# A two-layer decoder trunk on one core: first layer's parameter loads in three parts, weight sums started later

## The chip, the cores and the metric

One core of a Trainium2 chip. The metric is the device time of one execution in microseconds (us), as the median of several runs. A profile is one execution with the hardware profiler on. Its engines are PE (TensorE: matmuls and transposes), DVE (VectorE), ACT (ScalarE), POOL (GpSimd) and SP (SyncE, which here only issues transfers). Each of them works through its own queue in order and waits at the head of it for what its next instruction needs.

## The reference

Two layers, each with a residual connection, on x of 512 tokens by 1024 channels, all float32. One projection `w_in` feeds four groups; `w_out` joins them again.

```python
def hybrid_layer(x, positions, norm_g, w_in, ...):
    h = rmsnorm(x, norm_g)
    p = h @ w_in                                   # 1024 x 3488
    (cq, ckv, kr, g_a, c_h, c_b, c_c, g_b, sg_u, sg_v, g_c, mq, mk, mv, g_d) = jnp.split(p, offs, axis=-1)
    q  = rmsnorm(rmsnorm(cq, mla_q_norm_g) @ mla_w_uq, mla_q_g)          # 4 heads of 96
    kv = rmsnorm(ckv, mla_kv_norm_g) @ mla_w_ukv
    k_nope, k_rope = rmsnorm(..., mla_k_nope_g), rope(rmsnorm(kr, mla_k_rope_g))
    o_a = causal_attention_blocks(q, k, v_a)
    o_b = c_b * short_conv(c_c * c_h, conv_w)
    o_c = sg_u * (tril(sg_w) @ layernorm(sg_v, sg_ln_g, sg_ln_b) + sg_b)
    o_d = moba_attention(rope(rmsnorm(mq, moba_q_g)), rope(rmsnorm(mk, moba_k_g)), mv)
    y = concat([o_a * silu(g_a), o_b * silu(g_b), o_c * silu(g_c), o_d * silu(g_d)])
    return y @ w_out
```

## The kernel before

**Units.** The weights come in units of up to 128 x 1024 float32 (512 KB). `load_units` issues one transfer per unit on SP, in a fixed order: c0 to c3 (the columns cq, ckv and kr), uq, ukv, sq0 to sq3 (sg_v and mq), ga0, ga1 (a gate), kv0 to kv3 (mk and mv), su0, gc0, ch0, cc0 and so on. A unit lands in a raw buffer; there are two ordinary ones (`NRAW`), and c2, c3, uq, ukv and some later units use others, so sq0 gets the buffer of c0 and sq1 that of c1. `split_units` then splits each unit, half by half, in a high part (ACT, at times DVE) and a low part (DVE), and so frees the raw buffer. PE makes each product out of three matmuls (high x high, low x high, high x low). sq0 to sq2 are split into the tiles yTh and yTl, which are not otherwise used yet.

**Start.** In the first layer x is loaded in five pieces (`load_xk`), the last three of which `LOAD_HOOKS` puts behind the units c0 to c2. PE transposes it (xT), ACT scales it into hTh, DVE makes the low half hTl, and PE multiplies with c0 to c3 into cq (`c_first`). ACT also squares x for the norm (junk). The hook of ukv_0 calls `load_params(L0)`, which issues thirteen transfers for the first layer's small parameters: the gains cg (two), gq, gk, gr, lg, lb, dq, dk, the bias sgb and the convolution weights cw (three).

**Order.** All instructions are put out by a planner, `Order`, with a clock of its own: each chain of steps (`Chain`) asks to be resumed at a due time, and the steps of an engine go into its queue in the order in which the planner resumes them. Costs and due times are written in the code (`GT`, `MIXT`, `TS0` and others, in nanoseconds of that clock). On the chip only the order stays; when an instruction runs is decided by its queue and its semaphores. `scale`, which multiplies gq and dq by a constant on POOL, is due at `GT`, and `L.g_ev` tells the planner that both are done; `q_chain` and `mqk_chain` wait for it.

**Sums of output weights.** The last product of each layer (`seven`) is done with seven block products instead of eight, in the order b11, t3, b21, t4, t2, t1, b22. For that `t_sums` makes four sums of blocks of `w_out` in DRAM (t1 to t4), each in two halves: a copy, issued on SP, and a transfer that adds, issued on POOL.

```python
nc.sync.dma_start(z_src(l, n, j), z_src(l, a, j))
...
nc.gpsimd.dma_start(z_src(l, n, j), quad(l, b, j), accum_op=ALU.add, max_dma_last_dim=1024)
```

t1 and t3 come first, then t2 out of t1, then t4 out of t2. For the first layer it is started at `TS0`; for the second, after that layer's product sq. `load_units` loads t1 to t4 as units like any other, after they are made. The accumulators oz, ox and oy of the profile belong to this stage (oz: b11 and b21; ox: t3 and t4; oy: t2, t1, b22).

**Mix.** The spatial gate (`mix_chain`) has PE multiply the split of sg_w (wsh, wsl) with the normalized sg_v (vnh, vnl) into the tiles mp, between the matmuls of kv. ACT evicts them with the bias sgb into mix, which frees an accumulator of a pool of three.

Of the kernel before, what the change touches and what calls it, by code (L numbers as in the profile page):

```python
# [11 lines left out]
F32 = mybir.dt.float32  # L12
# [3 lines left out]
ALU = mybir.AluOpType  # L16
AX = mybir.AxisListType

P = 128
S = 512  # L20
NT = S // P
# [4 lines left out]
GW = 256  # L26
# [6 lines left out]
WSLACK = 0.0  # L33
AHEAD = 4
NWARM, FILL, FILLEND = 6, 0.9, 15000.0
MIXT, MIXLAG, ROWT, GT = 42000.0, 2000.0, 27000.0, 27000.0
KSPLIT, SQPOOL = 6, 700.0
PAIRS = {}
LOPRIO = -5
# [4 lines left out]
SEVEN = (0, 1)  # L44
K0, K1, KK = (2, 3, 0, 1), (4, 5, 6, 7), (0, 2, 3, 1)
ZPROD = ("b11", "t3", "b21", "t4", "t2", "t1", "b22")
TS0 = 36000.0
TAIL = ((0, 256), (256, 512))

C_CQ, C_KV, C_GA, C_CH, C_CB, C_CC, C_GB = 0, 256, 416, 672, 928, 1184, 1440  # L50
# [3 lines left out]
def dram(ap, offset, pattern):  # L54
    return bass.AP(tensor=ap.tensor, offset=ap.offset + offset, ap=pattern)
# [161 lines left out]
def hybrid_trunk(ctx: ExitStack, tc: tile.TileContext, x, positions, norm_g, w_c, w_f, w_t, w_o, mla_q_norm_g,  # L217
                 mla_w_uq, mla_kv_norm_g, mla_w_ukv, mla_q_g, mla_k_nope_g, mla_k_rope_g, conv_w,
                 sg_ln_g, sg_ln_b, sg_w, sg_b, moba_q_g, moba_k_g, out):
    nc = tc.nc  # L220
    V, A, G, PE = nc.vector, nc.scalar, nc.gpsimd, nc.tensor

    cst = ctx.enter_context(tc.tile_pool(name="cst", bufs=1))
    lay = ctx.enter_context(tc.tile_pool(name="lay", bufs=1))
# [13 lines left out]
    o = Order()  # L238
# [218 lines left out]
    LOAD_HOOKS = {}  # L457
# [103 lines left out]
    def bcast(src, offset, n, name):  # L561
        tl = lay.tile([P, n], F32, tag=name, name=name)
        nc.sync.dma_start(tl, dram(src, offset, [[0, P], [1, n]]))
        return tl
# [10 lines left out]
            L.ng.append(g)  # L575
        o.set(L.ng_ev, ch.t)

    def load_params(L):
        l = L.l
        L.cg = lay.tile([P, 384], F32, tag="cg_b", name="cg_b")  # L580
        nc.sync.dma_start(L.cg[:, 0:256], dram(mla_q_norm_g, l * 256, [[0, P], [1, 256]]))
        nc.sync.dma_start(L.cg[:, 256:384], dram(mla_kv_norm_g, l * 128, [[0, P], [1, 128]]))
        L.gq = bcast(mla_q_g, l * 96, 96, "gq_b")
        L.gk = bcast(mla_k_nope_g, l * 64, 64, "gk_b")
        L.gr = bcast(mla_k_rope_g, l * 32, 32, "gr_b")
        L.lg = bcast(sg_ln_g, l * GW, GW, "lg_b")
        L.lb = bcast(sg_ln_b, l * GW, GW, "lb_b")
        L.dq = bcast(moba_q_g, l * 64, 64, "dq_b")
        L.dk = bcast(moba_k_g, l * 64, 64, "dk_b")
        L.sgb = lay.tile([P, 4], F32, tag="sgb", name="sgb")  # L590
        nc.sync.dma_start(L.sgb, dram(sg_b, l * 512, [[1, P], [P, 4]]))
        L.cw = lay.tile([P, 2, 3], F32, tag="cw", name="cw")
        for j in range(3):
            nc.sync.dma_start(L.cw[:, :, j], dram(conv_w, (l * 3 + j) * GW, [[1, P], [P, 2]]))
        L.par_t = o.now + 4000.0
        L.ssq = lay.tile([P, NT, 3], F32, tag="ssq", name="ssq")
        L.krt = lay.tile([P, NT, 32], F32, tag="krt", name="krt")

        def scale():
            ch = Chain(o, L.par_t)  # L600
            yield from ch.pool(G.tensor_scalar, L.gq, L.gq, -(96 ** -0.5), None, op0=ALU.mult)
            yield from ch.pool(G.tensor_scalar, L.dq, L.dq, -0.125, None, op0=ALU.mult)
            o.set(L.g_ev, ch.t)
        o.spawn(scale(), None if L.l else GT, 2)

    layers = []
    for l in range(DEPTH):
        L = Layer()
        L.l = l
        L.ng_ev = Event()  # L610
        L.hT, L.hTh = [[Event(), Event()] for _ in range(NT)], [[Event(), Event()] for _ in range(NT)]
        if l:
            L.xss = [cst.tile([P, 4], F32, name=f"xss{t}_{l}") for t in range(NT)]
        L.qd = [Event() for _ in range(NT)]
        L.kd = [Event() for _ in range(NT)]
        L.stat = [Event() for _ in range(NT)]
        L.Vt, L.Mt, L.gates, L.gate_ev, L.MD = {}, {}, {}, {}, {}
        L.md_ev = {n: [Event() for _ in range(NT)] for n in ("mq", "mk", "mv")}
        L.vt_ev = [Event() for _ in range(NT)]
        L.y = [Event() for _ in range(KT)]  # L620
        L.xr = [Event() for _ in range(NT)]
        L.vn_ev = [Event() for _ in range(NT)]
        L.u, L.u_ev, L.b, L.b_ev = {}, {}, {}, {}
        L.mix_ev, L.mla_ev, L.QK_ev = Event(), Event(), Event()
        L.seven = l in SEVEN
        L.hT_free, L.p1, L.h_done, L.h = Event(), Event(), [Event(), Event()], {}
        L.s_done, L.g_ev = Event(), Event()
        L.s = {n: [Event() for _ in range(4)] for n in ("t2", "t1", "b22")}
        L.left, L.s4 = {}, [Event(), Event()]
        L.QK_taken = False  # L630
        L.torder = (2, 3, 0, 1) if l and layers[l - 1].seven else (0, 1, 2, 3)
        L.x = [None] * NT
        for n in ("ga0", "ga1", "gd0", "gd1"):
            L.gate_ev[n] = Event()
        for j in range(2):
            L.u_ev[j] = Event()
            L.b_ev[j] = [Event() for _ in range(3)]
        layers.append(L)
# [15 lines left out]
    def rv(i, t):  # L654
        return xv[:, i, t:t + 1]
# [505 lines left out]
    def mqk_chain(nm):  # L1161
        def f(L, t, a, t0, put):
            ch = Chain(o, t0)
            l = L.l
            gn = L.dq if nm == "mq" else L.dk
            if t == 0:
                L.MD[nm] = yield from ydS.get(ch, f"{nm}{l}", [P, NT, 4, 64], F32)
                o.set(L.md_alloc[nm], ch.t)
            yield from ch.wait(L.md_alloc[nm])
            dst = L.MD[nm]  # L1170
            a4 = a[:, 0:256].rearrange("p (h d) -> p h d", h=4)
            m = sm.tile([P, 8], F32, tag="m" if nm == "mq" else "mk", name=f"m{nm}{t}_{l}")
            yield from ch.act(A.activation, dst[:, t], a4, AF.Copy)
            put(ch)
            yield from head_sums(ch, m, dst[:, t], 64)
            if l == 0:
                yield from ch.wait(v_ev)
            yield from ch.pool(G.tensor_scalar, m[:, 0:4], m[:, 0:4], 64 * EPS if l else rv(RE64, t), 1.0 / 64,
                               op0=ALU.add, op1=ALU.mult)
            yield from pow_rstd(ch, m[:, 4:8], m[:, 0:4], 4)  # L1180
            yield from ch.wait(L.g_ev)
            for h in range(4):
                yield from ch.dve(V.scalar_tensor_tensor, dst[:, t, h, :], in0=dst[:, t, h, :],
                                  scalar=m[:, 4 + h:5 + h], in1=gn, op0=ALU.mult, op1=ALU.mult)
            yield from ch.wait(rope_ev)
            ce = cosT[:, t, :].rearrange("p (i two) -> p i two", two=2)[:, :, 0]
            se = sinT[:, t, :].rearrange("p (i two) -> p i two", two=2)[:, :, 0]
            yield from rope(ch, dst[:, t, :, 0:8], dst[:, t, :, 8:16], ce.unsqueeze(1).to_broadcast([P, 4, 8]),
                            se.unsqueeze(1).to_broadcast([P, 4, 8]), 4, 8, f"{nm}{t}{l}")
            o.set(L.md_ev[nm][t], ch.t)  # L1190
        return f
# [562 lines left out]
    L0 = layers[0]  # L1754

    def start():
        o.clk["D"] = 1000.0
        cw = Chain(o)
        for kp in range(KT // 2):
            xk[kp] = yield from v4S.get(cw, f"x{kp}_0", [P, NT, 2 * P], F32)  # L1760
        load_xk(0, 1)
        wp = yield from sS.get(cw, "warm")
        ones = one_box[0][:, 0:P].bitcast(F32)
        V.memset(ones, 1.0)
        A.activation(xsum[:, 0, 0:1], ones[:, 0:1], AF.Square, scale=D ** -0.5)
        o.fill = lambda: PE.matmul(wp[:, 0:P], ones, ones, start=True, stop=True)
        for _ in range(NWARM):
            o.fill()
        PE.transpose(wp[:, 256:256 + NT + KT], junk[0:NT + KT, P:2 * P], ident[0:NT + KT, 0:NT + KT])
        V.tensor_copy(pg, wp[:, 256:256 + NT + KT])  # L1770
        o.pe_end, o.fill_until = 3700.0, FILLEND
        o.clk["V"] = 3700.0

        def fill_end():
            o.fill_until = 0.0
            sS.put(Chain(o))
            return
            yield
        o.spawn(fill_end(), FILLEND, -9)
        LOAD_HOOKS["c0_0"] = (lambda: load_xk(2, 4),)  # L1780
        LOAD_HOOKS["c1_0"] = (lambda: load_xk(4, 6),)
        LOAD_HOOKS["c2_0"] = (lambda: load_xk(6, 8),)
        LOAD_HOOKS["ukv_0"] = (lambda: load_params(L0),)
        L0.par_t = 17500.0
        for u in order[:10]:
            u.wanted = True
        o.spawn(load_units(), None, 4)
        o.spawn(split_units(0, 4), None, LOPRIO)
        o.spawn(split_units(4, len(order)), None, 5)
        o.spawn(rope_tables(), 3700.0, 4)  # L1790
        o.spawn(x_stats(), None, 5)
        o.spawn(x_row(), ROWT, 5)
        o.spawn(main(), None, 10)
# [54 lines left out]
```

## Time and profile before

| | |
|---|---|
| median of 3 runs | 499.88 us (499.43 to 501.58) |
| the profiled execution | 501.79 us |
| its span in the profile | 500.1 us |
| PE busy | 489.4 us (98%) |
| DVE, ACT, POOL busy | 395.9, 314.9, 162.5 us |
| transfers | 81.98 MB, mean 164 GB/s |

How to read the rows: a row of the list of waits gives engine, line and tile that waited, what it waited for, the total in us, the count and the longest. A row of the timeline gives start, duration, engine, line, operation, output <- inputs; in brackets, how long the engine had been idle before it and what ended that. Line L174 is the planner's helper through which nearly all steps of ACT, DVE and POOL pass, L204 that of PE, L283 that of transfers, L343 and L349 are the copies and adds of the sums, L563, L581 to L594 the parameter loads. So one reads by tiles.

### The profile page before, as it was taken

How to read it: one execution, taken by the hardware profiler on the slowest of the kernel's cores; microseconds unless marked ns; L12 is line 12 of the kernel's file. 1: busy time of each engine (PE TensorE's matmuls, PEld its weight loads, DVE VectorE, ACT ScalarE, POOL GpSimd, SP SyncE). 2: the span in 40 equal slices, each digit the busy share in tenths (PEclk: the TensorE clock that was granted, in tenths of full speed). 3: DMA queues.
4: the chain of work that ended last, by engine and by line, in shares of the span. 5: the costliest groups of instructions: out<-in, count | busy, mean ns of one | idle time of the engine just before them, and what ended most of it. 6: DMA issues, size and time to landing. Idle time of an engine off the chain costs nothing.

```text
span 500.1 us, 7817 instructions
## 1 busy us (share of the span) xinstructions
PE 489.4 (98%) x2455; PEld 416.3 (83%) x2455; DVE 395.9 (79%) x1014; ACT 314.9 (63%) x918; POOL 162.5 (32%) x327
## 2 busy tenths in 40 slices
PE   9889998999999999999999999999999999999997
PEld 8888876888878888888888988888888888888886
DVE  3578995477989898789998789677888888665992
ACT  6679845475677776456656795565767776524640
POOL 7728993334532020010041478445441010000000
PEclk9989999999999999999999999999999999999999
DMA  8623639427457423796574323556439565474652
GB/s 276 217 85 128 235 91 230 139 85 126 150 147 183 133 65 130 237 306 198 175 269 133 118 84 128 210 128 126 101 111 252 190 158 117 147 274 173 223 179 98
DMA packets 37394, 81.98 MB, mean 164 GB/s; under 512 B 7133, under 2 KB 19433, under 8 KB 37097
## 3 DMA queue, kind: packets, MB, share of 16 engines
q1 hardware_dynamic: 28880, 73.09, 43.6%
q0 software_dynamic: 8448, 8.39, 11.1%
q8 instruction: 19, 0.31, 0.2%
q14 instruction: 23, 0.18, 0.1%
q10 hardware_dynamic: 24, 0.01, 0.0%
HBM read 73.61 MB, written 24.64 MB: 196 GB/s over the span
## 4 chain that ended last, share of the span: by engine, by line
PE 82%; DVE 7%; DMA 4%; ACT 3%; SPq 2%; issue 1%; POOL 0%; ACTq 0%
PE kv L204 9%; PE oy L204 6%; PE sq L204 5%; PE gb L204 4%; PE cb L204 4%; PE gd L204 4%; PE su L204 4%; PE oz L204 4%; PE ox L204 4%; PE cq L204 4%; PE cc L204 4%; PE gc L204 4%; PE ch L204 3%; PE sa L204 3%; PE ga L204 2%; PE sd L204 2%
## 5 line engine op out<-in xcount | busy, mean ns | idle before, releaser
L204 PE MATMUL kv<-whi_kv,hTh 128*128 128x512 f32 x64 | 27.0, 422 | 2.3 <-ACT mix L174 2.3
L174 ACT ACTIVATE pha<-pTa 128x512 fp32r<-128x512 f32 (+3 forms) x32 | 13.8, 435 | 23.9 <-PE pTa L204 23.9
L174 ACT ACTIVATE pd<-pd,mnd 128x256 f32<-128x256 f32 (+3 forms) x49 | 26.2, 545 | 2.9 <-DVE mnd L174 2.8
L174 ACT ACTIVATE pa<-pa,mna 128x256 f32<-128x256 f32 (+3 forms) x44 | 23.7, 549 | 4.4 <-DVE mna L174 4.4
L204 PE MATMUL kv<-wlo_kv,hTh 128*128 128x512 f32 x64 | 25.7, 401 | 0.0
L204 PE MATMUL kv<-whi_kv,hTl 128*128 128x512 f32 x64 | 25.6, 400 | 0.0
L174 ACT ACTIVATE phd<-pTd 128x512 fp32r<-128x512 f32 (+3 forms) x32 | 13.8, 435 | 17.4 <-PE pTd L204 17.3
L349 POOL DMA_DIRECT2D t<-in_w_o_dram x16 | 17.7, 1150 | 21.5 <-DMA t<-t 13.4
L204 PE MATMUL cq<-whi_c,hTh 128*128 128x416 f32 x64 | 21.8, 387 | 2.6 <-ACT hTh L174 2.6
L174 DVE TENSOR_TENSOR pla<-pTa,pha 128x512 fp32r<-128x512 f32 (+3 forms) x32 | 15.3, 482 | 9.4 <-ACT pha L174 9.3
L174 POOL TENSOR_TENSOR chs<-chs,rh 128x512 f32<-128x512 f32 x6 | 8.7, 1444 | 41.7 <-DVE chs L174 22.6
L174 DVE TENSOR_TENSOR wlo_t<-raw_t,whi_t 128x512 fp32r<-128x512 f32 x32 | 21.1, 681 | 0.0
L204 PE MATMUL cq<-wlo_c,hTh 128*128 128x416 f32 x64 | 20.6, 368 | 0.0
L204 PE MATMUL cq<-whi_c,hTl 128*128 128x416 f32 x64 | 20.4, 364 | 0.1
L174 ACT ACTIVATE whi_t<-raw_t 128x512 fp32r<-128x512 f32 x31 | 17.6, 618 | 3.8 <-DMA raw_t<-t 3.8
L174 DVE TENSOR_TENSOR pld<-pTd,phd 128x512 fp32r<-128x512 f32 (+3 forms) x32 | 15.5, 486 | 4.5 <-ACT phd L174 4.3
L204 PE MATMUL sq<-yTh,hTh 128*128 128x512 f32 x48 | 18.9, 393 | 0.0
L204 PE MATMUL sq<-yTh,hTl 128*128 128x512 f32 x48 | 18.7, 390 | 0.0
L204 PE MATMUL sq<-yTl,hTh 128*128 128x512 f32 x48 | 18.7, 389 | 0.0
L174 DVE CUSTOM_DVE_ANT_0 pa<-sa,maskb 128x512 f32<-128x512 f32 (+3 forms) x32 | 15.0, 482 | 3.6 <-PE sa L204 2.4
L174 DVE CUSTOM_DVE_ANT_0 pd<-sd,maskb 128x384 f32<-128x384 f32 (+3 forms) x32 | 15.2, 483 | 2.4 <-PE pTd L204 1.7
L174 DVE TENSOR_TENSOR wlo_b<-raw_b,whi_b 128x512 fp32r<-128x512 f32 x24 | 16.0, 684 | 1.2 <-ACT whi_b L174 1.2
(423 smaller groups left out, 1865.5 us busy)
## 6 DMA issues: line engine op xcount, KB each, us to landing
t<-in_w_o_dram POOLq DMA_DIRECT2D x16, 512.0 KB, 6.7
raw_t<-t SPq DMA_DIRECT2D x16, 512.0 KB, 4.2
raw_b<-in_w_o_dram SPq DMA_DIRECT2D x12, 512.0 KB, 4.4
raw_sq<-in_w_t_dram SPq DMA_DIRECT2D x8, 512.0 KB, 3.5
t<-in_w_o_dram SPq DMA_DIRECT2D x8, 512.0 KB, 5.3
raw_kv<-in_w_t_dram SPq DMA_DIRECT2D x8, 512.0 KB, 3.5
t<-t SPq DMA_DIRECT2D x8, 512.0 KB, 5.0
ys<-ysc SPq DMA_DIRECT2D x14, 256.0 KB, 5.7
```

What stands on the lines that cost most here:

```text
L174: f(*a, **k)
L204: f(*a, **k)
L349: nc.gpsimd.dma_start(z_src(l, n, j), quad(l, b, j), accum_op=ALU.add, max_dma_last_dim=1024)
```

## The change

`load_params` takes a part. For the first layer, part 0 (the two loads of cg) stays at ukv_0; part 1 (gr, gq, gk) is put behind the load of sq1, part 2 (lg, lb, dq, dk, sgb, cw) behind that of sq3. The scaling of gq stays due at `GT` (27 us of the planner's clock); the scaling of dq gets an event of its own, `gd_ev`, and is due at 42 us; `mqk_chain` waits for that. The second layer's parameters are loaded in one piece as before, with two chains for the scalings. `TS0` goes from 36 to 95 us.

```diff
-MIXT, MIXLAG, ROWT, GT = 42000.0, 2000.0, 27000.0, 27000.0
+MIXT, MIXLAG, ROWT, GT, GT2 = 42000.0, 2000.0, 27000.0, 27000.0, 42000.0
...
-TS0 = 36000.0
+TS0 = 95000.0
...
-    def load_params(L):
+    def load_params(L, part=None):
         l = L.l
...
+        if part in (None, 0):
+            L.cg = lay.tile([P, 384], F32, tag="cg_b", name="cg_b")
+            nc.sync.dma_start(L.cg[:, 0:256], dram(mla_q_norm_g, l * 256, [[0, P], [1, 256]]))
+            nc.sync.dma_start(L.cg[:, 256:384], dram(mla_kv_norm_g, l * 128, [[0, P], [1, 128]]))
+            L.ssq = lay.tile([P, NT, 3], F32, tag="ssq", name="ssq")
+            L.krt = lay.tile([P, NT, 32], F32, tag="krt", name="krt")
+            if l:
+                L.par_t = o.now + 4000.0
+        if part in (None, 1):
+            L.gr = bcast(mla_k_rope_g, l * 32, 32, "gr_b")
+            L.gq = bcast(mla_q_g, l * 96, 96, "gq_b")
+            L.gk = bcast(mla_k_nope_g, l * 64, 64, "gk_b")
+        if part in (None, 2):
+            L.lg = bcast(sg_ln_g, l * GW, GW, "lg_b")
+            L.lb = bcast(sg_ln_b, l * GW, GW, "lb_b")
+            L.dq = bcast(moba_q_g, l * 64, 64, "dq_b")
+            L.dk = bcast(moba_k_g, l * 64, 64, "dk_b")
+            L.sgb = lay.tile([P, 4], F32, tag="sgb", name="sgb")
+            nc.sync.dma_start(L.sgb, dram(sg_b, l * 512, [[1, P], [P, 4]]))
+            L.cw = lay.tile([P, 2, 3], F32, tag="cw", name="cw")
+            for j in range(3):
+                nc.sync.dma_start(L.cw[:, :, j], dram(conv_w, (l * 3 + j) * GW, [[1, P], [P, 2]]))
+
+        def scale(z, f, ev, t):
+            ch = Chain(o, t)
+            yield from ch.pool(G.tensor_scalar, z, z, f, None, op0=ALU.mult)
+            o.set(ev, ch.t)
+        if part in (None, 1):
+            o.spawn(scale(L.gq, -(96 ** -0.5), L.g_ev, L.par_t if l else GT), None, 2)
+        if part in (None, 2):
+            o.spawn(scale(L.dq, -0.125, L.gd_ev, L.par_t if l else GT2), None, 2)
...
-        L.s_done, L.g_ev = Event(), Event()
+        L.s_done, L.g_ev, L.gd_ev = Event(), Event(), Event()
...
-            yield from ch.wait(L.g_ev)
+            yield from ch.wait(L.gd_ev)
...
-        LOAD_HOOKS["ukv_0"] = (lambda: load_params(L0),)
+        LOAD_HOOKS["ukv_0"] = (lambda: load_params(L0, 0),)
+        LOAD_HOOKS["sq1_0"] = (lambda: load_params(L0, 1),)
+        LOAD_HOOKS["sq3_0"] = (lambda: load_params(L0, 2),)
```

More of the change, by code (lines that the diff above doesn't have):

```diff
@@ L576, in load_norm_gain @@
         o.set(L.ng_ev, ch.t)
-    def load_params(L):
+    def load_params(L, part=None):
         l = L.l
[L580 to L604, printed above, removed]
```

## The prediction

> **What bounds the kernel now.** I read the page's busy times and clock first, then who PE waited for, then the stretches around those waits.
>
> ```profile
> PE 489.4 (98%) x2455; PEld 416.3 (83%) x2455; DVE 395.9 (79%) x1014; ACT 314.9 (63%) x918; POOL 162.5 (32%) x327
> PEclk9989999999999999999999999999999999999999
> PE cq L204 <- ACT hTh L174: 2.6, 1, 2.6
> PE kv L204 <- ACT mix L174: 2.3, 1, 2.3
> PE warm L1766 <- DVE ones L1764: 1.1, 1, 1.1
> ```
>
> TensorE is busy for 489.4 of 500.1 us, so nothing outside its queue matters unless it makes PE wait or slows it. Only two waits of the whole run are longer than that of the warm-up at the start (1.1 us): one on the first projection (cq), one on the second token projection (kv). Each is followed by a second loss, which the busy share hides and of which the page's clock row, in tenths of 12.5 us slices, shows only one 8:
>
> ```profile
> 26.26:28.40 2.14, 2.00 (x6) 1.58 (x7) 2.00 (x4) 2.14 (x6) 0.00 (x0) 0.74 0.00 0
> 28.40:30.48 2.08, 2.08 (x7) 1.99 (x6) 1.56 (x5) 0.88 (x5) 0.00 (x0) 0.50 0.87 246
> 84.55:86.60 2.05, 2.05 (x6) 1.67 (x7) 1.28 (x7) 2.05 (x8) 0.00 (x0) 0.69 1.21 194
> 86.60:88.40 1.80, 1.80 (x6) 1.36 (x5) 1.54 (x5) 1.36 (x8) 0.31 (x1) 0.50 1.22 229
> ```
>
> These are the stretches just after the waits (after the length: busy time of PE, PEld, DVE, ACT, POOL; then the granted clock). PE is busy but granted 0.74 and 0.50, then 0.69 and 0.50 of full speed. The time lost is length times the missing clock: 0.26 x 2.14 + 0.50 x 2.08 = 1.6 us after the first wait, 0.31 x 2.05 + 0.50 x 1.80 = 1.5 us after the second. So wait A costs 2.6 + 1.6 = 4.2 us and wait B 2.3 + 1.5 = 3.8 us.
>
> **Who makes wait A.** ACT's, PE's and SP's own rows in order of time:
>
> ```profile
> 20.61 0.19 ACT L174 ACTIVATION_READ_ACCUMULATOR junk<-x 128x1 f32 x1
> 24.60 0.63 ACT L174 ACTIVATE yTh<-raw_sq 128x512 fp32r<-128x512 f32 x1 [3.80 <-DMA raw_sq<-in_w_t_dram]
> 25.54 0.67 ACT L174 ACTIVATE hTh<-xT,pg 128x512 fp32r<-128x512 f32 x1
> ...
> 21.09 0.60 PE L204 MATMUL xT<-ident,x 128*128 128x128 f32 x4
> 22.63 1.00 PE L204 MATMUL cq<-whi_c,hTl 128*128 128x416 f32 x4
> 26.26 0.46 PE L204 MATMUL cq<-whi_c,hTh 128*128 128x416 f32 x1 [2.62 <-ACT hTh L174]
> ...
> 9.00 0.33 SPq L581 DMA_DIRECT2D cg_b<-in_mla_q_norm_g_dram  x1
> 11.54 0.33 SPq L563 DMA_DIRECT2D gq_b<-in_mla_q_g_dram  x1
> 18.14 1.53 SPq L594 DMA_DIRECT2D cw<-in_conv_w_dram  x3
> 19.79 1.89 SPq L283 DMA_DIRECT2D raw_sq<-in_w_t_dram  x2
> ```
>
> hTh, the scaled transpose that PE needs, stands in ACT's queue behind the split of unit sq0, and ACT sat 3.80 us waiting for that unit. The unit was issued at 19.79 because SP first issued the parameters, from 9.00 on. It was usable 24.60 - 19.79 = 4.8 us later.
>
> **Part 1, the parameters.** After the change only the two cg loads stand ahead of sq0; eleven issues, from gq at 11.54 to the end of cw at 19.67, go behind sq1 (three) and sq3 (eight). sq0 takes gq's place, about 11.5, or some us later if its buffer or the full queue holds it. The buffers hold it little:
>
> ```profile
> 10.68 1.23 DVE L174 TENSOR_TENSOR wlo_c<-raw_c,whi_c 128x416 fp32r<-128x416 f32 x2 [1.29 <-ACT whi_c L174]
> ```
>
> This is the end of the split of c1, which frees sq1's buffer at 11.9; sq0's comes from c0, which is split before c1. At 11.5 + 4.8 = 16.3 sq0 lies 4.5 us ahead of ACT, which is ready for it at 20.80; so its issue may slip to 16 before anything is lost, and at worst, behind the full queue, it lands where it did. With the unit there, ACT goes from 20.80 through that half split (0.6 by its row) and a square and its read-out (25.54 - 24.60 - 0.6 = 0.3) to hTh at about 21.8, done at 22.5; its input, PE's transpose, is finished at 21.7, and PE's last matmuls before the wait run to 23.63. Nothing is then late by more than some tenths: the lower half of hTh is one more DVE step and PE wants it two matmuls later. All of A goes: 4.2 us, or 2.6 if the clock loss stays, or 0 if the landing stays late.
>
> What the three parts cost where they go, with their cover:
>
> ```profile
> 27.61 0.33 SPq L283 DMA_DIRECT2D raw_sq<-in_w_t_dram  x1
> 30.87 0.33 SPq L283 DMA_DIRECT2D raw_sq<-in_w_t_dram  x1
> 39.76 4.33 SPq L283 DMA_DIRECT2D raw_ga<-in_w_f_dram  x2
> L174 DVE SCALAR_TENSOR_TENSOR krt<-krt,ms,gr_b x8: 218/244/307, 38.7 to 294.4; 128x32 f32<-128x32 f32 x8
> L174 DVE SCALAR_TENSOR_TENSOR vn<-sq,bmv,lg_b x3: 471/471/472, 57.0 to 68.0; 128x256 f32<-128x256 f32 x3
> ```
>
> The three behind sq1 fit in SP's idle time before sq2 (27.61), and gr is first read at 38.7. The eight behind sq3 take 8 x 0.5 (cw's three took 1.53) to 8 x 0.83 us (gq to cw, 6.6 us for eight steps under a full queue), that is 4 to 6.6 us in a gap of 39.76 - 31.2 = 8.6 us, in which SP waits for a buffer anyway; lg, the first of them to be read, is wanted at 57.0. Cost 0; without that cover ga0 would move by up to 6.6 us, which has its own lead. All these rows move forward together when A goes. POOL's scaling of dq, now an instruction by itself after a later due time, is the same single operation. Cost 0.
>
> **Part 2, the sums.** Around wait B:
>
> ```profile
> 74.80 0.33 SPq L283 DMA_DIRECT2D raw_su<-in_w_f_dram  x1
> ...
> 71.78 2.34 POOL L349 DMA_DIRECT2D t<-in_w_o_dram  x2
> 81.55 1.21 POOL L349 DMA_DIRECT2D t<-in_w_o_dram  x1
> ...
> 82.62 0.63 ACT L174 ACTIVATE whi_su<-raw_su 128x512 fp32r<-128x512 f32 x1 [5.13 <-DMA raw_su<-in_w_f_dram]
> 84.03 1.19 ACT L174 ACTIVATE mix<-mp,sgb 128x256 f32<-128x256 f32 x3
> ...
> 79.91 0.28 PE L204 MATMUL mp<-vnh,wsl 128*128 128x256 f32 x1
> 84.55 0.50 PE L204 MATMUL kv<-whi_kv,hTh 128*128 128x512 f32 x1 [2.25 <-ACT mix L174]
> ...
> raw_kv<-in_w_t_dram SPq DMA_DIRECT2D x2, 512.0 KB, 3.5
> ```
>
> Same pattern: the mix evictions, which free PE's accumulator, stand in ACT's queue behind the split of su0, whose 512 KB took 82.62 - 74.80 = 7.8 us where kv units of that size take 3.5. POOL's adding transfers ran just then. Without them su0 is there at 78.3 plus tenths; the first mix tile is finished by PE at 80.2, and two evictions and one half split (0.4 + 0.6 + 0.4) end at 81.6. PE is ready at 84.55 - 2.25 = 82.3, so cover is 0.7 us. B goes: 3.8 us; 2.3 if only the wait goes, 0 if su0 is late for another reason.
>
> The eight copies and eight adds of layer 0 start 59 us later and meet other loads. What that costs is bounded by the lead of those loads:
>
> ```profile
> 142.46 0.33 SPq L283 DMA_DIRECT2D raw_ch<-in_w_f_dram  x1
> 151.60 0.62 ACT L174 ACTIVATE whi_ch<-raw_ch 128x512 fp32r<-128x512 f32 x1
> ```
>
> ch1 is split 9.1 us after its issue, so even su0's 7.8 us would fit: cost 0 there, 3.8 us if one load is caught as su0 was. Copies stand in SP's queue in front of loads that mostly wait for buffers; no gain below zero either, since PE does not wait in that stage.
>
> **The sum.** 4.2 + 3.8 = 8.0 us. The profiled execution took 501.79 us (span 500.1), 1.9 above the median; 501.79 - 8.0 = 493.8, and for the median 499.88 - 8.0 = 491.9.
>
> **The rivals.**
>
> *One stall stays or comes back elsewhere.* For it: the change of due times alters the planned order of ACT, DVE and POOL from there on, and DVE has no room in the stage before B:
>
> ```profile
> 62.50:75.00 12.50, 12.24 (x54) 9.86 (x53) 12.19 (x40) 5.29 (x18) 11.27 (x17) 1.00 0.31 91
> ```
>
> DVE is busy 12.19 of 12.50 us, and su0's issue waits for it. Against it: both waits have a named DMA as cause. Result 499.88 - 4 = 495.9.
>
> *The clock does not follow the waits.* By my reading the halved clock is caused by the wait, so it goes with it. If it is set by something else, only the waits go: 499.88 - 2.6 - 2.3 = 495.0. [...]
>
> *The sums become the bound, slower.* The last sum that layer 0 uses is t4:
>
> ```profile
> 44.14 0.60 SPq L343 DMA_DIRECT2D t<-in_w_o_dram  x1
> 153.82 1.03 POOL L349 DMA_DIRECT2D t<-in_w_o_dram  x1
> 229.94 2.18 ACT L174 ACTIVATE whi_t<-raw_t 128x512 fp32r<-128x512 f32 x4
> DMA to landing us min/median/max: 3.1/5.5/10.0
> ```
>
> Copies and adds ran from 44.14 to 153.82. Shifted by 59 us and forward by 4.2 (A) to 8.0, the last add is issued at 204.8 to 208.6 and lands 5.5 to 10.0 later (median and longest of the transfers on these tensors, the last row), at 210.3 to 218.6; the unit's load needs 3.5 more, 213.8 to 222.1. Its split now stands at 229.94 - 8.0 = 221.9, and SP's loads queue behind the waiting one. So it just fits. If it is X late there, PE loses X plus 1.6 of clock; the gain is gone at X = 6.4 and the kernel is 0.5% slower from X = 8.9. With X = 10: 499.88 - 8.0 + 11.6 = 503.5. Against it: the adds are not paced by the plan but go when their copies have landed, and later copies can catch up.
>
> *Nothing happens.* sq0 is held by the queue to 20.8 or later and su0 is late by DVE's backlog, or a gain is taken back: 498 to 501.
>
> **How the numbers follow.** Forecast 0.60 (own range 490.3 to 494); one stall left 0.17; clock independent 0.05; nothing 0.08; slower 0.10. A measurement of this kernel can tell about 0.5%, 2.5 us, from no change. Faster by more (under 497.4) holds the first three, 0.82; within it 0.08; slower 0.10. The range 490.0 to 497.2 takes in the forecast with all its bounds above and the cases at 495.0 and 495.9, and leaves out about 2 in 10.
>
> **What would show it.** In the changed profile: sq0's issue near 11.5 to 13; ACT's row yTh without the 3.80; the cq matmul without 2.62 and a clock of 1.00 from 20 to 40 us; adds on POOL absent from 60 to 90 and su0 usable some 4 us after issue; kv without its 2.25; the first copy near 100; whi_t without an idle on raw_t. It is wrong if PE's list of waits shows a new entry over 1 us between 30 and 240, if clock is below 1.00 without a wait, or if ACT's split of t4 waits for its DMA and PE (ox) for it.

## The result: 498.9 us against 500.5, and the profile after

The changed kernel takes 498.9 us (median of 16 runs, 497.13 to 500.23), the kernel before in the same series 500.54 (16 runs); the ratio is 0.9959 with a 95% interval of 0.9942 to 0.9977. By the medians 1.6 us are gained where 8.0 were forecast. The profiled execution took 499.82 us, its span is 498.1. Its mean granted clock is 0.997; so is that of 3 more of the 16 (median of the four 499.96), while the other 12 have 0.999 or 1.000 (median 498.68). This matters below, where a loss of clock is read from the profile.

First the page of the changed kernel: its busy times, the granted clock in 40 slices, and behind them the list of PE's waits up to 260 us.

```profile
PE 487.1 (98%) x2455; PEld 413.6 (83%) x2455; DVE 398.6 (80%) x1014; ACT 312.2 (63%) x905; POOL 168.8 (34%) x334
...
PEclk9999989999999999999999999999999999999999
...
PE ga L204 <- DVE vn L174: 1.8, 1, 1.8
PE cq L204 <- ACT hTh L174: 1.5, 3, 0.8
PE pTa L204 <- DVE pla L174: 1.3, 1, 1.3
PE warm L1773 <- DVE ones L1771: 1.1, 1, 1.1
PE oy L204 <- DVE xr L174: 0.7, 1, 0.7
PE oy L204 <- DVE suml L174: 0.5, 1, 0.5
```

In the kernel before, the list has these two at the end:

```profile
PE ga L204 <- DVE vn L174: 0.3, 1, 0.3
PE pTa L204 <- DVE pla L174: 0.2, 1, 0.2
```

Both waits of before are gone in their old form: cq's single 2.6 became three short ones of 1.5 together, kv <- mix is no longer there. But two others have grown past 1 us, ga <- vn and pTa <- pla, and there are two new ones on oy. The slice with the 8 in the clock row begins at 62 us, right behind the ga wait.

To see where the time went, the span is cut at three points of the matmuls: the first sq product (the end of the start), the first oz product (the begin of layer 0's last products) and the last oy product. Their rows, with first and last start, in the kernel before and then in the changed one:

```profile
L204 PE MATMUL sq<-yTh,hTh x24: 389/389/477, 33.5 to 61.8; 128*128 128x512 f32 x24
...
L204 PE MATMUL oz<-whi_b,yTh x12: 389/389/395, 218.3 to 234.0; 128*128 128x512 f32 x12
...
L204 PE MATMUL oy<-whi_b,yTh x8: 389/389/481, 251.0 to 256.7; 128*128 128x512 f32 x8
```

```profile
L204 PE MATMUL sq<-yTh,hTh x24: 389/389/496, 29.3 to 57.7; 128*128 128x512 f32 x24
...
L204 PE MATMUL oz<-whi_b,yTh x12: 389/389/389, 214.6 to 230.3; 128*128 128x512 f32 x12
...
L204 PE MATMUL oy<-whi_b,yTh x8: 389/389/481, 249.0 to 254.7; 128*128 128x512 f32 x8
```

The very last oy matmul (whi_b with yTl, behind the ones in the oy rows) starts at 257.1 before and at 255.2 in the change. In us:

| | start to first sq | middle: sq to oz | last products: oz to oy | rest |
|---|---|---|---|---|
| before | 33.5 | 184.8 | 38.8 | 243.0 |
| after | 29.3 | 185.3 | 40.6 | 242.9 |
| difference | -4.2 | +0.5 | +1.8 | -0.1 |

The start gained the whole of wait A, clock included. The middle lost wait B and is none the shorter (in this execution, one of the four with a mean clock of 0.997, lost behind ga here). The last products got longer. The rest is 242.9 to 243.1 in every kernel below and is left out from here on.

### The profile page after: what moved, and what is told of

Read it like the earlier page. It is cut to its first block, busy times and chain, and to the rows that moved or that the text cites. A ratio compares the mean times of both kernels' runs of the same rounds, so it can differ in the third digit from the quotient of the medians.

```text
span 498.1 us, 7805 instructions
## 1 busy us (share of the span) xinstructions
PE 487.1 (98%) x2455; PEld 413.6 (83%) x2455; DVE 398.6 (80%) x1014; ACT 312.2 (63%) x905; POOL 168.8 (34%) x334
## 4 chain that ended last, share of the span: by engine, by line
PE 83%; DVE 8%; ACT 3%; DMA 2%; issue 1%; SPq 1%; POOL 0%; DVEq 0%
PE kv L204 10%; PE cq L204 6%; PE sq L204 5%; PE oy L204 5%; PE ga L204 5%; PE gd L204 4%; PE gb L204 4%; PE cb L204 4%; PE gc L204 4%; PE su L204 4%; PE cc L204 4%; PE ch L204 3%; PE sa L204 3%; PE ox L204 2%; PE oz L204 2%; PE od L204 2%
## 5 line engine op out<-in xcount | busy, mean ns | idle before, releaser
L204 PE MATMUL cq<-whi_c,hTh 128*128 128x416 f32 x64 | 20.8, 371 | 1.5 <-ACT hTh L174 1.5
L174 DVE TENSOR_TENSOR wlo_b<-raw_b,whi_b 128x512 fp32r<-128x512 f32 x24 | 17.0, 731 | 2.3 <-ACT whi_b L174 2.2
L174 POOL TENSOR_SCALAR xss<-xss 128x1 f32<-128x1 f32 x4 | 2.8, 696 | 43.3 <-ACT jk L174 38.0
```

Source lines behind the costliest of these rows:

```text
L174: f(*a, **k)
L204: f(*a, **k)
```

## The experiments

All runs of one group stand beside runs of the kernel before on the same chip; ratios are to those, with the 95% interval. The stages are those of the profiled execution, which for e9 took 504.01 us, 2.1 above its median.

| kernel | due: dq scaling, sums | first sq | middle | last products | median us | ratio |
|---|---|---|---|---|---|---|
| e1_params_only | 27, 36 | 28.9 | 182.4 | 38.8 | 495.29 | 0.9908 (0.9881 to 0.9934) |
| e1b_params_rec | 42, 36 | 29.5 | 183.4 | 38.8 | 496.26 | 0.9913 (0.9892 to 0.9933) |
| e2_sums95 | as before, 95 | 35.5 | 182.0 | 42.0 | 503.83 | 1.0066 (1.0046 to 1.0087) |
| e3_both_keep | 27, 95 | 28.8 | 182.1 | 42.1 | 497.34 | 0.9934 (0.9913 to 0.9955) |
| e5_after_dq27 | 27, 95 | 28.9 | 182.1 | 41.9 | 497.63 | 0.9923 (0.9894 to 0.9951) |
| e4_e1_ts75 | 27, 75 | 28.6 | 180.7 | 38.7 | 492.92 | 0.9832 (0.9804 to 0.9860) |
| e10_e1_ts65 | 27, 65 | 29.0 | 181.7 | 38.7 | 493.88 | 0.9839 (0.9812 to 0.9867) |
| e4_e1_ts115 | 27, 115 | 29.2 | 181.5 | 47.9 | 504.43 | 1.0070 (1.0041 to 1.0100) |
| e6_pars_after_t4 | 27, 95 | 29.1 | 182.2 | 43.5 | 499.80 | 0.9971 (0.9953 to 0.9989) |
| e8_e3_ys_first | 27, 95 | 28.7 | 182.1 | 44.3 | 500.79 | 0.9980 (0.9962 to 0.9999) |
| e9_after_ys_first | 42, 95 | 29.3 | 185.3 | 44.8 | 501.95 | 1.0017 (0.9994 to 1.0041) |
| e11_t4_raw | 27, 95 | 28.5 | 182.2 | 43.0 | 497.13 | 0.9914 (0.9895 to 0.9934) |
| e12_no_t4 | 27, 95 | 28.5 | 182.1 | 40.2 | 495.78 | 0.9890 (0.9871 to 0.9909) |

### Each part by itself

**e1_params_only**: the parameter parts alone, with both scalings in one chain due at 27 us, so that every queue but SP's has the order of before.

```diff
-TS0 = 95000.0
+TS0 = 36000.0
...
-        def scale(z, f, ev, t):
-            ch = Chain(o, t)
-            yield from ch.pool(G.tensor_scalar, z, z, f, None, op0=ALU.mult)
-            o.set(ev, ch.t)
+        def scale():
+            ch = Chain(o, L.par_t)
+            yield from ch.pool(G.tensor_scalar, L.gq, L.gq, -(96 ** -0.5), None, op0=ALU.mult)
+            yield from ch.pool(G.tensor_scalar, L.dq, L.dq, -0.125, None, op0=ALU.mult)
+            o.set(L.g_ev, ch.t)
+            o.set(L.gd_ev, ch.t)
```

> Only the three parts of the parameter loads are moved; both scalings stay in one chain due at 27 us and the sums start at 36 us, so the queues of PE, DVE, ACT and POOL hold the same instructions in the same order as in the kernel before. Theory 1 (DVE is full in the sq stage whatever its order): the first sq matmul comes 4.2 us earlier, near 29.3 us, and then ga waits for DVE for 1.5 to 2 us with a half clock of 1.5 us behind it, so that 1 us or less of the gain reaches kv; time 0.998 of before. Theory 2 (the wait at ga in the changed kernel is made by another order of DVE's queue, not by DVE's load): all rows from 33 to 82 us move forward by 4.2 us, no wait at ga; the wait at kv stays (su0 still meets the adds); time 0.9915 of before (4.2 us of 500).

**e1b_params_rec**: the parameter parts as in the change, dq's scaling due at 42 us; only `TS0` is put back to 36000.

> The parameter part of the change as it was made, with the later due time of dq's scaling, and the sums at 36 us as before. Against e1 it differs by the planned order that follows from that due time. Theory 1: as e1. Theory 2: if the later due time of dq alters DVE's order, ga waits as in the changed kernel (1.8 us and the clock behind it) and this kernel is some 3 us slower than e1; if it is the sums' start that does it, this kernel is as fast as e1.

**e2_sums95**: the kernel before with `TS0 = 95000` and nothing else.

> Only the start of the sums is moved, from 36 to 95 us; the parameters are loaded as before. Both theories: the first wait (cq, 2.6 us and a half clock) is unchanged; the kv wait for mix (2.3 us and 1.5 us of clock) is gone; near 215 us SP's load of t4 waits for the add, the ys loads behind it are late, and oy loses 1.2 to 2 us. Net 0.996 of before (2 us). If the new order of DVE alone makes the wait at ga, there is one here too, 1 to 3 us, and the kernel is as slow as before or slower.

**e3_both_keep**: e1_params_only with `TS0 = 95000`.

> Both parts, but with the scalings due as before, so that the queues of PE, DVE, ACT and POOL hold the order of e2. Theory 1: ga waits 1.5 to 2 us with its half clock, gain 8.0 - 3.3 - 1.8 = 3 us, 0.994 of before. Theory 2: if the order of e2 has no wait at ga, the gain is 8.0 - 1.8 = 6 us, 0.988.

Theory 1 fell, Theory 2 holds: e1 has no long wait at ga and gains 0.9908, as Theory 2 said. The 0.9934 of e3 is near Theory 1's number, but not by its mechanism: its ga wait is 0.3, and what it lacks went to the last products (3.3 us longer instead of 1.8) and to two waits named below. PE's first ga product in the change and in e1, with its wait in brackets, and the stretches around it in the change (length, busy PE, PEld, DVE, ACT, POOL, then the granted clock):

```profile
61.77 0.56 PE L204 MATMUL ga<-hTh,whi_ga 128*128 128x512 f32 x1 [1.84 <-DVE vn L174]
...
59.74 0.47 PE L204 MATMUL ga<-hTh,whi_ga 128*128 128x512 f32 x1 [0.27 <-DVE vn L174]
```

```profile
61.00:62.00 1.00, 0.23 (x1) 0.27 (x2) 1.00 (x4) 0.01 (x1) 0.91 (x3) 1.00 0.00 0
62.00:65.40 3.40, 3.40 (x9) 2.63 (x9) 2.95 (x12) 2.90 (x12) 1.87 (x3) 0.50 0.00 0
65.40:66.40 1.00, 1.00 (x5) 0.80 (x5) 1.00 (x6) 0.00 (x0) 0.91 (x3) 0.99 0.17 45
```

Behind its wait the change loses 0.50 x 3.4 = 1.7 us of clock; so in this execution the stall costs 3.5 us, of which 0.3 was there before. In the 12 executions without a loss of clock it can cost only the wait. In e1b the same wait is 1.88 with no loss of clock behind it, and e1b is only 1.0 us slower than e1 by the medians (the intervals overlap), not the 3 us that were expected. e1, with the queues of PE, VectorE, ScalarE and GpSimd in the old order, does not have the wait, though PE arrives there 0.5 us sooner still (59.47 against 59.93).

Why the order changes: `rope` asks the planner whether VectorE's clock plus 400 ns is still behind GpSimd's (or the chain's own time, if that is later), and takes VectorE if so. With the later scaling of dq the first rope falls just on the other side: in the planner's nanoseconds it is 43 454 + 400 against 43 765 in the kernel before, and 42 817 + 400 against 43 217, by less than 1, in the change. VectorE's rows of the change show the work that came in, ahead of the second vn that PE needs:

```profile
47.95 0.21 DVE L174 TENSOR_TENSOR rbk<-krt,sinT 128x64 f32<-128x64 f32 x1
...
50.89 0.20 DVE L174 TENSOR_TENSOR krt<-krt,cosT 128x64 f32<-128x64 f32 x1
...
55.91 0.22 DVE L174 TENSOR_TENSOR rbq<-Q,sinT 128x64 f32<-128x64 f32 x1
...
59.61 0.21 DVE L174 TENSOR_TENSOR Q<-Q,cosT 128x64 f32<-128x64 f32 x1
...
61.15 0.47 DVE L174 SCALAR_TENSOR_TENSOR vn<-sq,bmv,lg_b 128x256 f32<-128x256 f32 x1
```

Before its second vn VectorE has ten such rope steps in the change and none in e1; the second vn starts at 59.12 in e1 and at 61.15 in the change.

e2 was forecast faster and came 0.66% slower. Its middle is 2.8 shorter than before, so wait B is indeed the sums' work, but the last products are 3.2 longer, and wait A was 3.6 us in its profile instead of 2.6 (its sq0 was issued at 20.70 instead of 19.79, though the queues up to there are those of before; why is not settled). The half clock behind it lasts 6.8 us, where the kernel before has 3.4. e3 shows the same 42.1 in the last products.

What the sums do to wait B is shown by the row of su0's split on ACT, behind which mix waits, in e1 (sums at 36) and in e3 (sums at 95):

```profile
77.26 0.63 ACT L174 ACTIVATE whi_su<-raw_su 128x512 fp32r<-128x512 f32 x1 [4.27 <-DMA raw_su<-in_w_f_dram]
...
73.78 0.63 ACT L174 ACTIVATE whi_su<-raw_su 128x512 fp32r<-128x512 f32 x1 [0.93 <-DMA raw_su<-in_w_f_dram]
```

su0 was issued at 70.30 and 70.17: usable after 7.0 us beside the adds, after 3.6 without them. Yet in e1 the kv wait is only 1.4 us (2.25 before) with the clock at 1.00 behind it, so the parameter parts alone had taken 2.4 of the 3.8 us of B, 1.5 of it clock (in 4 of e1's 6 executions; the other two have a mean clock of 0.996 and 0.997). What was left for the sums' move was 1.4; the middle of e3 is 0.3 shorter than e1's, since two waits of 0.9 and 0.6 (pTd, tmqd) come with its order.

### dq's due time put back in the change

**e5_after_dq27**:

```diff
-MIXT, MIXLAG, ROWT, GT, GT2 = 42000.0, 2000.0, 27000.0, 27000.0, 42000.0
+MIXT, MIXLAG, ROWT, GT, GT2 = 42000.0, 2000.0, 27000.0, 27000.0, 27000.0
```

> The whole change with one number put back: the scaling of dq is due at 27 us again instead of 42 (its load stays behind sq3). Theory 2 (dq's later due time turned the planner's choice for the first rope from GpSimd to VectorE, and that put work ahead of the second vn): the entry ga <- DVE vn, 1.8 us after the change, falls under 0.5; the stretch from the first sq product to the first oz product falls from 185.3 to about 182.2; the last product stage of layer 0 keeps its 42 us; time about 497.2, ratio to before 0.993. Rival (VectorE is full in that stage with any order, or the load behind sq3 is too late): the ga wait stays near 1.8 and the time at about 498.9, ratio 0.996.

One number takes the ga wait to 0.3 and the middle from 185.3 to 182.1, as expected. That the ratio moves only from 0.9959 to 0.9923 has two reasons: the last products are 41.9 instead of 40.6 in this order, and 1.7 of the 3.2 us are the clock that, by a mean of 0.997, only 4 of the change's 16 executions lose.

### The last products: when the sums come

**e4_e1_ts75** and **e4_e1_ts115**: e1_params_only with `TS0 = 75000` and `115000`; **e10_e1_ts65** later with `65000`.

> Parameters in three parts with one scaling chain due at 27 us, and the sums due at 75 us instead of 36 or 95. Theory 3 (late sums cost only because t4's adding transfers land after its load is wanted): 20 us earlier than with 95, t4's adds are issued before layer 1's parameter loads, the wait of the load queue for t, 10.1 us with 95, is gone, the stage from the first oz product to the last oy product is 38.8 to 39.3 as with 36 instead of 42.1, and the middle stage keeps 182.1 to 182.6; time 494.6 to 495.6, ratio 0.989 to 0.991. Rival (the sums cost wherever they meet other loads, and 95 is only one such place): a stage between gets longer by 1 us or more, time 496.5 to 498.

> The same with the sums due at 115 us. Theory 3: t4's adds come about 20 us later than with 95, and each microsecond of that holds the load queue and the products of t4: the stage from the first oz to the last oy product grows from 42.1 to between 50 and 62, time 505 to 517. Rival (the 3.3 us of that stage with 95 are lost to traffic of the sums beside its loads, not to t4's lateness): the stage stays within 2 us of 42.1, time 496 to 499.

> Parameters in three parts with one scaling chain, sums due at 65 us (75 gave 492.9). Theory 4: the stage from the first oz to the last oy product stays at 38.8, since t4 is landed long before; what the middle stage does is not forecast closely, since the planned order of VectorE and ScalarE between 85 and 210 us is another one again: 180.5 to 183; time 492.5 to 495.5. Rival (10 us earlier the sums already meet the load of su0 near 70 us, as with 36): a wait kv <- ACT mix over 0.5 us comes back.

With the sums due at 36, 65 and 75 the stage is 38.7 or 38.8, with 95 it is 40.6 (the change) to 42.1, with 115 it is 47.9: flat up to 75, then growing. In e4_e1_ts75 and e10_e1_ts65 kv has no wait, so 65 is late enough for su0. e4_e1_ts115 came out below what was expected, and PE's wait there is plainly t4 (ox <- whi_t, 3.5 us, with 6.8 us of clock at 0.50 behind it). e4_e1_ts75 came out faster than expected, at 492.9 us: beside the 38.7 its middle is 180.7, 1.7 shorter than e1's; 1.4 of this is the kv wait, which e1 still has and e4_e1_ts75 has not. It is the best version, 1.7% faster than before. Its page has no wait over 1 us but that of the warm-up, and no slice of the clock below 9:

```profile
PE 485.5 (99%) x2455; PEld 413.9 (84%) x2455; DVE 392.9 (80%) x1000; ACT 314.8 (64%) x913; POOL 169.7 (35%) x340
...
PEclk9999999999999999999999999999999999999999
```

Its planned order of the middle differs from e1's and from e3's: it also has none of e3's waits of 0.9 and 0.6 at pTd and tmqd. Which step of the order spares these was not tried.

### The last products: why 95 is too late

SP's own list of waits in the change, 170 to 245 us, and SP's and POOL's rows for t4:

```profile
SPq L283 <- DMA t<-in_w_o_dram: 7.7, 1, 7.7
...
197.12 0.48 SPq L343 DMA_DIRECT2D t<-t  x1
...
216.89 0.32 SPq L283 DMA_DIRECT2D raw_t<-t  x1
217.30 2.75 SPq L283 DMA_DIRECT2D ys<-ysc  x6
...
205.85 0.79 POOL L174 TENSOR_SCALAR gq_b<-gq_b 128x96 f32<-128x96 f32 x1 [5.93 <-DMA gq_b<-in_mla_q_g_dram]
...
208.34 1.07 POOL L349 DMA_DIRECT2D t<-in_w_o_dram  x1
...
210.84 1.04 POOL L349 DMA_DIRECT2D t<-in_w_o_dram  x1
```

Three suspects can be read from this: the scaling of layer 1's gq, which stands in front of the adds on POOL; the load of t4 (raw_t at 216.89), which holds SP for 7.7 us with the six loads of ys behind it; and the traffic. ys are the parts of y that VectorE and ScalarE add and split into the sums sumh and suml for the oy products. The runs below were made against one suspect each.

**e6_pars_after_t4**: e3 with layer 1's parameters held until the adds are issued.

```diff
         yield from ch.wait(L.b_ev[1][1])
+        if L.seven:
+            yield from ch.wait(tsum_ev[L.l, "t4", 1])
         load_params(layers[L.l + 1])
```

> Parameters in three parts with one scaling chain, sums due at 95 us, and layer 1's parameter loads (and their scalings on GpSimd) held until t4's adds have been issued. Theory 3 (t4's adds stand on GpSimd behind the scaling of gq for layer 1, which waits 4.6 us for its load): the adds are issued about 5 us sooner, the load queue's wait for t falls from 10.1 to about 5, and the stage from the first oz to the last oy product from 42.1 to 39 to 40.5; time 494.8 to 496.3, ratio 0.989 to 0.992. Rival (the adds are late because their own chain of copies is late; the scaling adds nothing): the stage stays at 42, time 497.3, ratio 0.993.

SP's wait for t fell to 2.7, but the thirteen parameter issues now stood between t4's load and ys, whose issue came at 218.8, and the stage grew to 43.5. So with the adds no longer behind the scaling the stage was not shorter, but since the issues took its place in front of ys, this run does not show what the scaling alone is worth; the rival of this expectation did not foresee the growth either.

**e8_e3_ys_first** and **e9_after_ys_first**: e3 and the change with one instruction moved, the load of t4's first half behind the six of ys.

```diff
-                dma(ch, P * n * 4, u.raw[:, :n], u.src)
+                dma(ch, P * n * 4, u.raw[:, :n], u.src, held if u.name == "t40_0" else None)
...
             dma(c2, P * 2048, w[-1], ysc[L.l][kt])
+            ys_n.append(kt)
+            if len(ys_n) == 6:
+                nc.sync.dma_start(*held)
```

> Parameters in three parts with one scaling chain and the sums due at 95 us, with one instruction moved in one queue: the load of t4's first half is issued behind the six ys loads instead of ahead of them; every other queue has the same order. Theory 4 (what the late sums cost is the lateness of the ys loads, which stand on the load queue behind a load that waits for t4's adding transfer): the ys loads are issued near 204 instead of 214.5, that is 7 us ahead of the first oz product instead of 3.6 behind it, and the stage from the first oz to the last oy product falls from 42.1 to about 39; time 494 to 495, ratio 0.987 to 0.990. Rival (t4's own late landing, or its split on VectorE and ScalarE, sets that stage): the stage stays at 41.5 to 42.5 and new waits appear at ox; time 497.3, ratio 0.993.

> The change as it is, with that one instruction moved in the load queue. Theory 4: the stage from the first oz to the last oy product falls from 40.6 to about 38.8; the ga wait of 1.8 us stays; time 497.0, ratio to before 0.992 to 0.994. Rival: no difference from the change, 498.9, ratio 0.996.

Theory 4 fell: the stage got longer in both, 44.3 and 44.8. VectorE's rows say why; e3 first, then e8:

```profile
220.72 0.42 DVE L174 TENSOR_TENSOR ys<-ys,ys 128x256 f32<-128x256 f32 x1 [2.33 <-DMA ys<-ysc]
221.06 0.68 DVE L174 TENSOR_TENSOR wlo_t<-raw_t,whi_t 128x512 fp32r<-128x512 f32 x1
...
225.14 0.68 DVE L174 TENSOR_TENSOR suml<-ys,sumh 128x512 fp32r<-128x512 f32 x1
```

```profile
218.21 0.42 DVE L174 TENSOR_TENSOR ys<-ys,ys 128x256 f32<-128x256 f32 x1
223.20 0.69 DVE L174 TENSOR_TENSOR wlo_t<-raw_t,whi_t 128x512 fp32r<-128x512 f32 x1 [4.57 <-ACT whi_t L174]
...
227.28 0.68 DVE L174 TENSOR_TENSOR suml<-ys,sumh 128x512 fp32r<-128x512 f32 x1
```

With ys there early, VectorE does one step of it and then stands 4.57 us at the split of a t unit, which the plan put between the steps of ys. The queue needs both loads; whichever lands last ends the hole, and in e8 that was 2.1 us later.

**e11_t4_raw**: the change with dq at 27 us, and the two t4 loads of layer 0 reading weights that are always there, so that nothing waits for the sum. **e12_no_t4**: the same without t4's four transfers.

```diff
-                    add_unit(z_src(l, n, j), 2, 512, f"{n}{j}_{l}")
+                    add_unit(quad(l, "b21", j) if (l, n) == (0, "t4") else z_src(l, n, j), 2, 512, f"{n}{j}_{l}")
```

```diff
-                    nc.sync.dma_start(z_src(l, n, j), z_src(l, a, j))
+                    if (l, n) != (0, "t4"):
+                        nc.sync.dma_start(z_src(l, n, j), z_src(l, a, j))
...
-                    nc.gpsimd.dma_start(z_src(l, n, j), quad(l, b, j), accum_op=ALU.add, max_dma_last_dim=1024)
+                    if (l, n) != (0, "t4"):
+                        nc.gpsimd.dma_start(z_src(l, n, j), quad(l, b, j), accum_op=ALU.add, max_dma_last_dim=1024)
```

> The change with dq's scaling due at 27 us again, and the two loads of t4 in layer 0 read the raw output weights instead of the sum (so layer 0's product with t4 is made with other weights; the transfers that form t4 stay where they are, and every queue has the same instructions in the same order). Theory 5 (the plan puts t4's splits ahead of the ys work on VectorE and ScalarE, and in order of their queues both then wait for t4's loads, which wait for its adding transfers; the later this hole of VectorE ends, the longer the stage): the hole that ended 9.6 us behind the first oz product is gone or ends under 6 us behind it, the stage from the first oz to the last oy product falls from 41.9 to 38.8 to 39.5, time 494 to 495, ratio 0.986 to 0.989. Rival (the planned order of the queues itself costs the stage, with the data there or not): the stage stays over 41, time 497, ratio 0.992.

> As the kernel before it in this list (the change with dq's scaling due at 27 us, layer 0's product with t4 made from the raw weights), and the four transfers that form t4 of layer 0, two copies and two adds, are left out; all other instructions stand in the same order on every queue. Theory 6 (it is the traffic: t4's copies and adds, moved to 187 to 220 us, share the 16 DMA engines, at a share of 1.05 to 1.12 between 204 and 224, with the loads of the last product stage, so the ys loads land late and VectorE's hole ends 10.7 us behind the first oz product): the hole is gone or ends at most 6.5 us behind it, the DMA share in that stretch falls under 1.0, the stage from the first oz to the last oy product falls from 43.0 to 38.8 to 39.5, time 493 to 494.5, ratio 0.984 to 0.988. Rival (the planned order of VectorE and ScalarE costs the stage, whatever the transfers do): the hole ends over 8 us behind, the stage stays over 41, time 496 to 497.

e11: without any wait for t4 the hole stays and the stage is 43.0, so the wait was not it (Theory 5, as put, fell; its rival named the order and is half right, as e12 shows). e12: without the transfers VectorE's longest idle time from 216 to 220 us is 0.91 us and the stage is 40.2, where 38.8 to 39.5 was expected. SP's issue of the six ys loads and the windows, e11 then e12 (the last two columns are DMA share and GB/s):

```profile
207.91 7.03 SPq L283 DMA_DIRECT2D ys<-ysc  x6
...
208.00:212.00 4.00, 4.00 (x21) 3.31 (x20) 2.44 (x4) 0.42 (x1) 0.00 (x0) 1.00 1.12 289
...
216.00:220.00 4.00, 4.00 (x20) 3.30 (x19) 1.23 (x2) 1.51 (x3) 0.00 (x0) 1.00 1.09 331
```

```profile
207.86 2.76 SPq L283 DMA_DIRECT2D ys<-ysc  x6
...
208.00:212.00 4.00, 4.00 (x22) 3.30 (x21) 2.49 (x4) 0.48 (x1) 0.00 (x0) 1.00 0.76 261
...
216.00:220.00 4.00, 4.00 (x19) 3.30 (x18) 3.10 (x7) 2.16 (x4) 0.00 (x0) 1.00 0.81 240
```

Beside t4's copies and adds the DMA share is 1.12 and 1.09 in these stretches instead of 0.76 and 0.81, the six issues alone take 7.03 us instead of 2.76, ys lands late, and VectorE is busy 1.23 of 4 us at 216 where it is busy 3.10 without them. So the traffic is worth 2.8 us of this stage against e11, and together with the wait for t4 1.7 us against e5, which has the same order and both. The 1.4 us left above 38.8 are there with no late transfer of t4 at all: by elimination that is the planned order, in which splits of t and evictions stand between the steps of ys; no run changed that order alone. e4_e1_ts75, where the plan expects t4 in time and so puts ys first, has its first suml at 216.05, 6.8 us behind its first oz.

One measure holds all of it together: the time from the first oz product to VectorE's first suml. It is 7.4 us before, 6.8 in e1, e1b, ts65 and ts75, and the stage is 38.7 to 38.8. From 12.4 us on the stage grows one for one (no run lies between 7.4 and 12.4; drawn back, the line meets 38.8 near 11): 12.4 us in e12 (stage 40.2), 12.7 in the change (40.6), 14.0 to 14.2 in e5, e2 and e3 (41.9 to 42.1), 15.2 in e11 (43.0), 15.7 in e6 (43.5), 16.5 in e8 (44.3), 17.0 in e9 (44.8). Only e4_e1_ts115 stands apart (8.5 and 47.9), where t4 itself holds ox. The change's own share of order and traffic was not parted by a run; its ys work was held 0.81 us by the transfer, in this row:

```profile
222.91 0.43 DVE L174 TENSOR_TENSOR ys<-ys,ys 128x256 f32<-128x256 f32 x1 [0.81 <-DMA ys<-ysc]
```

## Why the prediction was right or wrong

- **Wait A goes, 4.2 us: right, and in full.** sq0 was issued at 12.27 (forecast 11.5 to 13), its split runs at 21.30 with no wait, and the first sq product comes 4.2 us sooner: 2.8 at the wait and 2.0 behind it, where the clock is now 1.00, less 0.6 for the three short waits ahead of it. The change's rows of SP and ACT:

```profile
12.27 1.37 SPq L283 DMA_DIRECT2D raw_sq<-in_w_t_dram  x2
14.74 0.33 SPq L563 DMA_DIRECT2D gr_b<-in_mla_k_rope_g_dram  x1
...
21.30 0.62 ACT L174 ACTIVATE yTh<-raw_sq 128x512 fp32r<-128x512 f32 x1
```

- **The eleven moved loads cost 0: right.** In e1 no wait points to them.
- **dq's scaling "is the same single operation. Cost 0": this step failed.** Its duration is indeed nothing, 0.37 us on GpSimd. But the due time is an input of a planner, and one rope changed engines. In the change that made a wait of 1.8 us, with 1.7 us of clock behind it in the profiled execution (3 more of the 16 have its mean clock, 0.997), at the start of the VectorE stage whose lack of room the first rival named. Put back (e5), the middle is 3.2 us shorter by the profiles; between e1b and e1, where neither profile loses clock there, the same order costs 1.0. The rival had the mechanism; it priced it at one stall, and there was a second loss beside it. The forecast's own sign of being wrong, a new entry over 1 us in PE's list, came true twice, at ga and pTa.
- **Wait B goes, 3.8 us: the cause was right, the size of the sums' part was not.** su0's slow load beside the adds is shown (7.0 against 3.6 us). But in the profiles 2.4 of the 3.8 went with the parameters alone, in e1, so that B's price depended on A; the sum took the two as independent. The sums' move by itself, with A still there, gained 2.8 us in the middle.
- **The sums "meet other loads, cost 0": this step failed.** It looked at one unit, ch1, and at t4's landing against its own split. The row that it took for that split, 229.94, is that of t4's second half (and t2's first); t4's first half is split from 227.69 on, so there was 2.3 us less room than it counted. The last add was issued at 210.84, where 204.8 to 208.6 was forecast. t4's first half was loaded from 216.89 on, for a landing that the forecast put between 213.8 and 222.1, and still ox is not in the list of waits. The loss of 1.8 us came by another way: ys, loaded in the same stretch, and the planned order of VectorE, which put splits of t into the midst of the ys work. In the order of e3 it is 3.3 us.
- **The clock follows the waits: in part, and it was charged in full.** In the profiles, A, B and the ga wait of the change, 1.84 us, each have one stretch of 3.4 us at half clock behind them, 1.7 us; the forecast's 1.6 and 1.5 come from stretches cut a little short. The same wait in e1b, 1.88 us, kept 1.00, as did 1.4 on kv in e1. The kernel before does not lose the same in every execution either: of the 71 that stand beside the experiments, 46 have a mean clock of 0.993 or less, 23 of 0.996 or 0.997, 2 of 0.999 or more, with medians of 501.8, 500.2 and 499.2 us; at 1.7 us of 500 for each stretch that would be two or more, one and none, an estimate. The forecast took the clock of both stretches from a profiled execution 1.9 us above the median and subtracted it from the median.
- **The sum.** Forecast -4.2 and -3.8. Measured by the two profiles: start -4.2; middle +0.5, which is -3.8 for B, +1.5 for the longer wait at ga (0.3 before), +1.7 for the clock behind it and +1.1 for pTa (0.2 before); last products +1.8; rest -0.1; together -2.0, and -1.6 between the medians. In the 12 executions of the change without the 1.7 us of clock, 6 of the 8 us are missing all the same (median 498.68 against 500.54). The 8 us were there to be had: with dq's scaling at 27 and the sums at 75, ratio 0.9832 (0.9804 to 0.9860), which is 8.4 us of 500; by its profile the start is 4.9 us shorter and the middle 4.1.

## What to carry to other kernels

Where a planner writes the queues' order, a due time is not a local edit: compare the order of every queue before and after, and where it changed, cost the order and not the instruction. A transfer that is moved out of the way of one load can go into the way of others (here su0 was usable 3.6 us after its issue instead of 7.0, and the six loads of ys took 7.03 us to issue instead of 2.76): read the DMA share of the stretch where it lands, and what stands behind its readers in each queue, before calling it free. And try the parts of a change one by one: here the parameters alone were faster than both parts together, and the sums alone slower than no change at all.

## What the runs showed of the hardware

- The half clock behind a wait of PE came or stayed away as a whole in the profiles here. Between the start and the end of the kernel it lasted 3.4 us at 0.50 (both waits before, ga in the change) or 6.8 us (cq in e2, ox in e4_e1_ts115), so it cost 1.7 us where PE was busy throughout, or up to 3.4. Which waits bring it is not settled by their length: 1.84 us (the change, ga) did, 1.88 at the same place (e1b) did not, and neither did two of 1.9 and 1.2 within 4 us (e9, ox, clock 1.00 from 228 to 236 us). Why the two runs of the ga wait differ, no run here shows. The row of the kernel before behind wait A, that of e2 behind the same wait, and the rows of e1b behind ga:

```profile
27.30:30.70 3.40, 3.40 (x11) 3.23 (x11) 2.73 (x6) 2.17 (x8) 0.00 (x0) 0.50 0.54 154
...
26.40:33.20 6.80, 5.54 (x16) 5.05 (x17) 5.24 (x11) 4.93 (x18) 0.60 (x1) 0.50 0.28 78
...
60.00:62.50 2.50, 0.62 (x3) 0.48 (x3) 2.50 (x13) 0.27 (x1) 2.31 (x4) 1.00 0.00 0
62.50:65.00 2.50, 2.50 (x12) 2.03 (x11) 2.05 (x9) 2.44 (x12) 1.79 (x4) 1.00 0.00 0
```

- A load of 512 KB (su0) was usable 7.0 us after its issue beside GpSimd's adding transfers (e1) and 3.6 us without (e3), and six loads of 256 KB (ys) took 7.03 us to issue at a DMA share of 1.12 (e11) against 2.76 at 0.76 (e12, both shares of 208 to 212 us): here the price of traffic showed in the issuing queue too.
